# Latent attention: a depthwise convolution as 128x32 products of four shifted copies, interleaved with the attention's head groups

## The chip, the cores and the metric

The kernel runs on one core of a Trainium2 chip. The engines of the core work side by side, each with an instruction queue of its own that is executed in order: TensorE (PE) multiplies and transposes, VectorE (DVE), ScalarE (ACT) and GpSimd (POOL) do elementwise work, SyncE (SP) issues most of the DMAs. The metric is the device time of one execution in microseconds (us), as the median of several runs.

## The reference

Two transformer blocks of width 1024, one after the other, over 256 tokens in float32: a token mixer with a feed-forward part and a mixture of experts (MoE), twice a pair; then, in two layers, a feed-forward part, a mixing part and a second feed-forward part, and a norm. The change touches the mixing part of these two layers:

```python
p = h @ w_in[l]                                   # 384 + 256 + 32 + 2 * 512 columns
attn = mla_group(p[..., :o_kv], p[..., o_kv:o_pe], p[..., o_pe:o_cv], ...)
conv = conv_group(p[..., o_cv:], ...)
x = x + concatenate([attn, conv], axis=-1) @ w_out[l]
...
def mla_group(c_q_raw, c_kv_raw, k_pe_raw, ...):  # 8 heads, 64 + 32 of q and k, 64 of v
    q = (rms_norm(c_q_raw, q_lat_g) @ w_uq).reshape(b, s, 8, 96)
    kv = (rms_norm(c_kv_raw, kv_lat_g) @ w_ukv).reshape(b, s, 8, 128)
    # k = 64 of kv with the 32 of k_pe_raw for every head; q, k normed per head; rope on the 32
    # causal by chunks of 64: softmax(q k / sqrt(96)) v
def conv_group(u_raw, conv_w, conv_b, ln_g, ln_b):
    u = a * sigmoid(g)                            # the two halves of u_raw
    y = causal depthwise convolution of u, 31 taps, 512 channels, + conv_b
    return silu(layer_norm(y, ln_g, ln_b))
```

## The kernel before

The program goes through ten stages in this order: mix0, ffn0, mix1, moe, f1_0, mla0, f2_0, f1_1, mla1, f2_1. mla0 and mla1 are the mixing parts above; f1 and f2 are the feed-forward parts around them. Tokens lie in two tiles of 128 (t = 0, 1), X being the residual.

**Weights.** All of them are streamed from HBM by SP, in the order of `plan_...`, as blocks of 1 MB into a ring of four (`raw`); each block is cut into a high part `wh` by ACT (L237) and a low part `wl` by DVE (L238). A projection (`mul`) makes three products for each: high by high, low by high, high by low (L395, L396, L398), 128x128 of activations against up to 512 columns of weights. Activations are cut in the same way (`cut2`: ACT makes the high part `xhl`, DVE the low one). Before a stage the residual is transposed and cut and a reciprocal root of its mean square is made by `rstd_of`: two POOL instructions, L378 (add) and L379 (power). Behind the MoE there is one norm more: DVE scales X by that root (L440, `Norm.turn`), and only then X is transposed, cut and projected.

**Order.** A scheduler in the tile framework sets the order in each engine's queue from the order in which the code is written and from priorities (`tc.high_priority`), and puts the waits where data or buffers need them. It may put an instruction far ahead of where it is written, if its inputs and its buffer are there. A tile of PSUM (`bank`) or of SBUF that is asked for under a name in use makes its first writer wait for the last reader of the old one.

**A mixing stage** (`mla`) projects `ca` and `cg` (the two halves of u), `cq`, `ck` (latents of q and of k, v), then `uq` and `ukv` from the normed latents; q and k are normed per head (squares on ACT, sums on DVE, root on POOL), q's and k's last 32 columns are rotated by `rope` (L765 to L770, six products and sums on POOL for each t), heads are transposed by PE (L880) and moved by ACT; scores (L910, L911), exponentials (ACT L919), transposes of them (L404), values (L926). The out projection takes the attention half first and then the convolution's half, whose layer norm and silu (L946 to L956) are placed beside the first.

**The convolution** works on `uT`, u transposed to channels on partitions (four chunks of 128 channels) with 30 zero columns ahead. Chunks 0 and 1 and 26 taps of chunk 2 are done by DVE, one instruction a tap (`tap`, L788, L790). The remaining 5 taps and chunk 3 are 36 products of PE with a 128x128 diagonal that ACT makes from the identity for each tap (`pe_conv`, L796, L797). All of it has a low priority.

## Time and profile before

| | us |
|---|---|
| median of 3 runs | 2318.45 (2315.61 to 2323.34) |
| the profiled execution | 2321.03 |
| its span from first to last instruction | 2319.3 |
| mla0 and mla1, from the first to the last product of each | 134.3 and 131.6 |
| PE busy over the span | 2238.7 (97%) |
| DVE, ACT, POOL busy over the span | 926.1, 792.6, 172.7 |

Times in the rows are from the span's start. PE's products are pipelined, so a product's time overlaps with the next, and a busy PE isn't a PE at its full rate: the granted clock (PEclk, 1.00 is 2.4 GHz, 0.50 is 1.2 GHz) stands beside it. A float32 product leaves two records. The median of the runs is 2.6 us below the profiled execution, from which all rows come.

### The profile page before, as it was taken

How to read it: one execution, taken by the hardware profiler on the slowest of the kernel's cores; microseconds unless marked ns; L12 is line 12 of the kernel's file. 1: busy time of each engine (PE TensorE's matmuls, PEld its weight loads, DVE VectorE, ACT ScalarE, POOL GpSimd, SP SyncE). 2: the span in 40 equal slices, each digit the busy share in tenths (PEclk: the TensorE clock that was granted, in tenths of full speed). 3: DMA queues.
4: the chain of work that ended last, by engine and by line, in shares of the span. 5: the costliest groups of instructions: out<-in, count | busy, mean ns of one | idle time of the engine just before them, and what ended most of it. 6: DMA issues, size and time to landing. Idle time of an engine off the chain costs nothing. (4 is left out here: it accounts for less than half of the span.)

```text
span 2319.3 us, 36153 instructions
## 1 busy us (share of the span) xinstructions
PE 2238.7 (97%) x15276; PEld 1482.4 (64%) x15276; DVE 926.1 (40%) x1246; ACT 792.6 (34%) x1243; POOL 172.7 (7%) x258
## 2 busy tenths in 40 slices
PE   8999999899999999998999999989999999989998
PEld 7888888523433333333332688877888888867887
DVE  6655456201010101011010655586554645686544
ACT  5444444201010101101010544475444544575443
POOL 3000003000000000000000200061000100150000
PEclk9999999899999999999999999999999999999999
DMA  7655554899979999999999655441555555423552
GB/s 269 226 187 182 184 208 156 321 420 419 412 321 388 399 418 419 420 418 420 420 409 415 226 190 185 141 146 65 199 182 183 182 192 186 142 108 119 184 188 82
DMA packets 89436, 599.09 MB, mean 258 GB/s; under 512 B 12092, under 2 KB 14558, under 8 KB 18460
## 3 DMA queue, kind: packets, MB, share of 16 engines
q1 hardware_dynamic: 88956, 595.81, 66.2%
q8 instruction: 144, 2.36, 0.4%
q10 hardware_dynamic: 288, 0.52, 0.1%
q14 instruction: 48, 0.39, 0.0%
HBM read 595.25 MB, written 1.05 MB: 257 GB/s over the span
## 5 line engine op out<-in xcount | busy, mean ns | idle before, releaser
L238 DVE TENSOR_TENSOR wl<-raw,wh 128x1024 fp32r<-128x1024 f32 (+2 forms) x456 | 540.5, 1215 | 431.1 <-ACT wh L237 430.7
L237 ACT ACTIVATE wh<-raw 128x1024 fp32r<-128x1024 f32 (+2 forms) x456 | 454.6, 1036 | 485.8 <-PE mm L398 302.1
L1098 PE MATMUL mm<-raw,xe 128*32 128x512 f32 (+1 forms) x5376 | 506.8, 524 | 5.9 <-DMA raw<-in_w_moe_dram 5.1
L395 PE MATMUL mm<-wh,xhl 128*128 128x512 f32 (+3 forms) x1280 | 473.2, 372 | 2.3 <-ACT xhl L414 2.3
L396 PE MATMUL mm<-wl,xhl 128*128 128x512 f32 (+3 forms) x1280 | 471.5, 371 | 0.0
L398 PE MATMUL mm<-wh,xhl 128*128 128x512 f32 (+3 forms) x1280 | 394.4, 371 | 0.3 <-DVE xhl L415 0.3
L1098 PEld LDWEIGHTS mm<-raw,xe 128*32 128x32 f32 x5376 | 168.9, 110 | 301.5 <-issue 245.2
L1103 DVE TENSOR_TENSOR gs<-mm,gs 128x256 f32<-128x256 f32 (+1 forms) x84 | 31.2, 380 | 669.8 <-ACT gs L1102 420.9
L1126 PE MATMUL acc<-raw,gT 128*32 128x512 f32 (+1 forms) x2688 | 280.6, 523 | 12.4 <-DMA raw<-in_w_moe_dram 4.1
L395 PEld LDWEIGHTS mm<-wh,xhl 128*128 128x128 f32 x1280 | 241.8, 189 | 43.3 <-ACT xhl L414 2.7
L396 PEld LDWEIGHTS mm<-wl,xhl 128*128 128x128 f32 x1280 | 241.7, 189 | 40.9 <-DVE wl L238 0.6
L398 PEld LDWEIGHTS mm<-wh,xhl 128*128 128x128 f32 x1280 | 236.9, 189 | 41.5 <-DVE xhl L415 1.5
L1102 ACT ACTIVATE gs<-mm 128x256 f32<-128x256 f32 (+1 forms) x84 | 29.3, 349 | 516.3 <-PE mm L1098 516.3
L1126 PEld LDWEIGHTS acc<-raw,gT 128*32 128x32 f32 x2688 | 90.0, 109 | 168.2 <-issue 128.3
L395 PE MATMUL acc<-wh,ghl 128*128 128x512 f32 x464 | 186.0, 401 | 0.0
L396 PE MATMUL acc<-wl,ghl 128*128 128x512 f32 x464 | 183.4, 395 | 0.0
L398 PE MATMUL acc<-wh,ghl 128*128 128x512 f32 x464 | 145.3, 393 | 0.0
L378 POOL TENSOR_SCALAR s<-s 128x1 f32<-128x1 f32 (+1 forms) x60 | 32.3, 539 | 1156.5 <-ACT junk L385 1052.6
L398 PEld LDWEIGHTS acc<-wh,ghl 128*128 128x128 f32 x464 | 87.3, 188 | 20.7
L396 PEld LDWEIGHTS acc<-wl,ghl 128*128 128x128 f32 x464 | 87.6, 189 | 19.0
L395 PEld LDWEIGHTS acc<-wh,ghl 128*128 128x128 f32 x464 | 87.5, 189 | 18.7
L1112 ACT ACTIVATE gT<-mm 128x256 f32<-128x256 f32 (+1 forms) x84 | 29.1, 347 | 202.7 <-PE mm L1110 201.4
(254 smaller groups left out, 1633.0 us busy)
## 6 DMA issues: line engine op xcount, KB each, us to landing
raw<-in_w_moe_dram SPq DMA_DIRECT2D x336, 1024.0 KB
raw<-in_w_f_dram SPq DMA_DIRECT2D x132, 1024.0 KB
raw<-in_w_ffn_dram SPq DMA_DIRECT2D x42, 1024.0 KB
raw<-in_w_mix_dram SPq DMA_DIRECT2D x23, 1024.0 KB
raw<-in_w_mla_dram SPq DMA_DIRECT2D x18, 1024.0 KB
raw<-in_w_mla_dram SPq DMA_DIRECT2D x8, 576.0 KB
raw<-in_w_mla_dram SPq DMA_DIRECT2D x4, 768.0 KB
c<-in_cst_dram SPq DMA_DIRECT2D x2, 1024.0 KB
```

Source lines behind the costliest of these rows:

```text
L237: self.nc.scalar.activation(h[:, s], t, AF.Copy)
L238: self.nc.vector.tensor_tensor(l[:, s], t, h[:, s].bitcast(F32), op=ALU.subtract)
L378: nc.gpsimd.tensor_scalar(r, ms, EPS, None, ALU.add)
L395: nc.tensor.matmul(o, sh[:, k, :], h[:, j, a:b], start=first and i == 0, stop=False)
L396: nc.tensor.matmul(o, sh[:, k, :], l[:, j, a:b], start=False, stop=False)
L398: nc.tensor.matmul(o, sl[:, k, :], h[:, i + (r[0] if r else 0), a:b], start=False, stop=last and i == n - 1)
L1098: nc.tensor.matmul(ps[32 * j:32 * j + 32, :n], xe[e // 2][:, k, e % 2, 32 * g:32 * g + 32], units[k // 2][0](k % 2, c * n, n), start=k == ...
L1102: nc.scalar.activation(s, v[:, :, 0], AF.Silu)
L1103: nc.vector.tensor_tensor(s, v[:, :, 1], s, op=ALU.mult)
L1112: nc.scalar.activation(a, ps[:, :n * 128].rearrange("p (q c) -> p q c", q=n), AF.Copy)
L1126: last = nc.tensor.matmul(o[32 * j:32 * j + 32, :w], a[:, k % n, at:at + 32], units[k // 2][0](k % 2, c * w, w), start=b == 0 and k == 0, ...
```

## The change

The order of the projections becomes cq, ck, ca, uq, ukv, cg, and the convolution's half of the out projection comes first. The convolution moves to PE altogether. `uT` has no zero columns any more and lies in the scratch tile `junk`; SP copies it by 40 DMAs a layer, from SBUF to SBUF, into `us`: for each group of 32 channels a tile with those channels four times over its 128 partitions, each copy shifted by one token more. One product of a 128x32 weight with 256 columns then sums four taps of 32 channels, and eight products a group make the 32 taps (the first is zero). The four groups of a chunk go to the four column strips of the array. The weights (`taps`, 128x1024 a chunk, four chunks a layer, two buffers) are made on POOL from a sum of the identity's four blocks (`eye`) and the taps, which the host lays out (`cw` is loaded, not transposed at the start). The result `cv` goes into the scratch tile that `uT` had, by ACT. `rope` goes from POOL to DVE, as does one scaling of the norms; the copy of the transposed exponentials (`pT`) goes from ACT to DVE. Scores, values and the four parts of the convolution are written out as one interleaved list.

```diff
-        cols(("ca", l), w, 672, 512, D, 512)
-        cols(("cg", l), w, 1184, 512, D, 512)
         cols(("cq", l), w, 0, 384, D, 512)
         cols(("ck", l), w, 384, 288, D, 512)
+        cols(("ca", l), w, 672, 512, D, 512)
         for i in range(2):
             add((("uq", l), i), ("w_uq_2", (l,)), 0, 384, 384 * i, 384)
         add((("ukv", l), 0), ("w_ukv_2", (l,)), 0, 256, 0, D)
-        for i in range(4):
+        cols(("cg", l), w, 1184, 512, D, 512)
+        for i in (2, 3, 0, 1):
...
-        c["uT"] = pool.tile([128, 4, T + TAPS - 1], F32, name="uT")
-        nc.gpsimd.memset(c["uT"][:, :, 0:TAPS - 1], 0.0)
...
+        eye = c["eye"] = pool.tile([128, 32], F32, name="eye")
+        nc.gpsimd.tensor_tensor(eye, ident[:, 0:32], ident[:, 32:64], op=ALU.add)
+        for i in (2, 3):
+            nc.gpsimd.tensor_tensor(eye, eye, ident[:, 32 * i:32 * i + 32], op=ALU.add)
...
+    def taps_of(l, i, c, pool):
+        n = [128, 32, 32]
+        d = pool.tile(n, F32, tag="taps", name="taps", bufs=TABLES)
+        nc.gpsimd.tensor_tensor(d, c["eye"].unsqueeze(1).to_broadcast(n), cw[:, l, i].unsqueeze(2).to_broadcast(n), op=ALU.mult)
+        return d
...
-        e = nc.gpsimd
+        e = nc.vector
...
-        def pe_conv(i, k0):
-            ps = bank("acc")
-            for k in range(k0, TAPS):
-                d = pool.tile([128, 128], F32, tag="diag", name="diag", bufs=4)
-                nc.scalar.activation(d, ident, AF.Copy, scale=cw[:, l, i, k:k + 1])
-                nc.tensor.matmul(ps[:, :T], d, uT[:, i, k:k + T], start=k == k0, stop=k == TAPS - 1)
-            if k0:
-                nc.vector.tensor_tensor(cv[i], ps[:, :T], cv[i], op=ALU.add)
-            else:
-                nc.scalar.activation(cv[i], ps[:, :T], AF.Identity, bias=gain("conv_b_2", l)[:, i:i + 1])
...
-                with tc.high_priority(offset=-600):
-                    for k in range(TAPS):
-                        for j in range(3):
-                            if j < 2 or k < SPLIT:
-                                tap(j, k)
-                    pe_conv(2, SPLIT)
-                    pe_conv(3, 0)
...
+        ps_g = project(("cg", l), 2, nin, 512, K2, "acc")
+        gated = []
+        for t in range(2):
+            b = tp.tile([128, 512], F32, tag="g32", name="ug", bufs=4)
+            nc.scalar.activation(b, ps_g[t], AF.Sigmoid, scale=nin.r[t])
+            nc.vector.scalar_tensor_tensor(b, ps_a[t], nin.r[t], b, ALU.mult, ALU.mult)
+            gated.append(b)
...
+        wide = T + 28
+        us = [(xp.tile([128, UNIT], F32, tag="x", name="us")[:, :7 * wide].rearrange("p (g t) -> p g t", g=7),
+               pool.tile([128, 1, wide], F32, name=f"us{i}")) for i in range(2)]
+        for u in us:
+            for v in u:
+                nc.gpsimd.memset(v[:, :, 0:31], 0.0)
+        uT = tp.tile([128, 4, T], F32, tag="junk", name="uT", bufs=1)
+        for t in range(2):
+            p = turn4([gated[t][:, j * 128:(j + 1) * 128] for j in range(4)])
+            if t:
+                nc.vector.tensor_copy(uT[:, :, t * 128:(t + 1) * 128], p)
+            else:
+                nc.scalar.activation(uT[:, :, t * 128:(t + 1) * 128], p, AF.Copy)
+        for i in range(2):
+            for s in range(4):
+                n = min(T, wide - 31 + s)
+                for g in range(4):
+                    a = uT[32 * g:32 * g + 32, 2 * i:2 * i + 2, :n]
+                    k = 1 if g == 3 else 2
+                    nc.sync.dma_start(us[i][0][32 * s:32 * s + 32, 2 * g:2 * g + k, 31 - s:31 - s + n], a[:, :k])
+                    if g == 3:
+                        nc.sync.dma_start(us[i][1][32 * s:32 * s + 32, :, 31 - s:31 - s + n], a[:, 1:])
+
+        def group(i, g):
+            n = 2 * g + i % 2
+            return us[i // 2][0][:, n] if n < 7 else us[i // 2][1][:, 0]
+
+        def conv(i):
+            tab = taps_of(l, i, c, pool)
+            if i % 2 == 0:
+                sums.append(bank("acc"))
+            o = sums[i // 2][:, (i % 2) * T:(i % 2 + 1) * T]
+            for m in range(8):
+                for g in range(4):
+                    nc.tensor.matmul(o[32 * g:32 * g + 32], tab[:, 8 * g + m], group(i, g)[:, 4 * m:4 * m + T], start=m == 0, stop=m == 7)
+            nc.scalar.activation(cv[:, i // 2, i % 2], o, AF.Identity, bias=gain("conv_b_2", l)[:, i:i + 1])
...
-                nc.scalar.activation(pT, pp, AF.Copy)
...
+            nc.vector.tensor_copy(pT, pp)
...
+        css = quarters(F32)[0]
+        scores(0, 0)
+        cv = tp.tile([128, 2, 2, T], F32, tag="junk", name="cv", bufs=1)
+        conv(0)
+        scores(0, 1)
+        heads_T(kT, kf[1], 1, 1)
+        conv(1)
+        values(0, 0)
+        scores(1, 0)
+        values(0, 1)
+        a0 = weighted(0)
+        conv(2)
+        scores(1, 1)
+        conv(3)
+        values(1, 0)
+        b0 = conv_norm(0)
+        scores(1, 2)
+        attended(0, a0)
+        values(1, 1)
+        b1 = conv_norm(1)
+        scores(1, 3)
+        conv_out(0, b0)
+        values(1, 2)
+        conv_out(1, b1)
+        out_conv(0)
+        values(1, 3)
+        a1 = weighted(1)
+        out_conv(1)
+        attended(1, a1)
+        finish([(("wo2", l), 0), (("wo2", l), 1)], y, ch, cl, [range(0, 2), range(2, 4)], nout)
```

What the scheduler makes of it shows at three places.

POOL around the end of moe and the start of f1_0, before: `s_19671` is the mean square of X for t = 1, L378 and L379 make its root, on which DVE's scaling of X waits.

```order
L743 MEMSET neg 1x64
L745 MEMSET low 1x64
L746 MEMSET low 1x64
L756 MEMSET uT 128x4x30
L378 TENSOR_SCALAR s_19671<-s_19668 128x1
L379 TENSOR_TENSOR s_19671<-s_19671,mhalf 128x1
L754 TENSOR_TENSOR rot<-c_81,rg 128x16 x16
```

POOL there now; the same root is that of `s_19664` (lines L382, L383).

```order
L747 MEMSET neg 1x64
L749 MEMSET low 1x64
L750 MEMSET low 1x64
L761 TENSOR_TENSOR eye<-c_81 128x32
L887 MEMSET us_21565 128x31
L887 MEMSET us_21567 128x31
L763 TENSOR_TENSOR eye<-eye,c_81 128x32 x2
L769 TENSOR_TENSOR taps<-eye,cw 128x1024
L382 TENSOR_SCALAR s_19664<-s_19661 128x1
L769 TENSOR_TENSOR taps<-eye,cw 128x1024
L383 TENSOR_TENSOR s_19664<-s_19664,mhalf 128x1
L758 TENSOR_TENSOR rot<-c_81,rg 128x16 x16
```

Between the constants and the root now stand the sums for `eye`, two memsets of `us` and the first two tables; the second table is between the root's two halves.

SP at the end of mla0's weights, before: the last blocks of mla0, the first of f2_0 (`in_w_f_0`), then two small loads for mla1.

```order
L217 DMA raw<-in_w_mla_dram 128x1536 x2
L217 DMA raw<-in_w_mla_dram 128x1152 x4
L217 DMA raw<-in_w_mla_dram 128x2048 x5
L217 DMA raw<-in_w_f_0_dram 128x2048 x3
L741 DMA rg<-in_q_norm_dram 128x32
L741 DMA rg<-in_k_norm_dram 128x32
L217 DMA raw<-in_w_f_0_dram 128x2048 x2
```

SP there now, as far as the first half of the copies (an `x3` row is three DMAs).

```order
L226 DMA raw<-in_w_mla_dram 128x2048 x7
L226 DMA raw<-in_w_f_0_dram 128x2048 x2
L901 DMA us<-uT 32x2x253 x3
L901 DMA us<-uT 32x253
L903 DMA us_21565<-uT 32x253
L901 DMA us<-uT 32x2x254 x3
L901 DMA us<-uT 32x254
L903 DMA us_21565<-uT 32x254
L901 DMA us<-uT 32x2x255 x3
L901 DMA us<-uT 32x255
L903 DMA us_21565<-uT 32x255
L901 DMA us<-uT 32x2x256 x3
```

The copies stand in one row behind the first two blocks of f2_0; the other half follows in the same form (`us_21567`), and all of f2_0's later blocks behind it.

PE in mla0 where the convolution runs, before, in the middle of the heads: `diag` are products of the convolution, `kv,t32` values, `gn` transposes of exponentials, `kT,qT` scores.

```order
L797 MATMUL acc<-uT,diag 128x256 x2
L926 MATMUL acc<-kv_21585,t_21849 128x64 x4
L797 MATMUL acc<-uT,diag 128x256 x2
L404 MATMUL mm<-c_81,gn 128x128 x2
L910 MATMUL mm<-kT_21725,qT_21723 128x256
L404 MATMUL mm<-c_81,gn 128x128 x2
L911 LDWEIGHTS low
L911 MATMUL mm<-neg,low 128x64
```

PE now, with the numbers of the buffers: `us_21564` is the first set of copies (chunks 0 and 1) and `us_21566` the second (chunks 2 and 3); the `taps` are those of chunk 0 (`21646`), 2 (`21785`) and 1 (`21710`); `acc_21648` is the bank of chunks 0 and 1.

```order
L916 MATMUL acc_21648<-us_21564,taps_21646 32x256 x30
L916 MATMUL acc_21787<-us_21566,taps_21785 32x256 x2
L975 MATMUL acc_21866<-kv0_21292,t32_21872 128x64
L975 MATMUL acc_21866<-kv1_21293,t32_21872 128x64
L916 MATMUL acc_21787<-us_21566,taps_21785 32x256
L975 MATMUL acc_21866<-kv0_21292,t32_21872 128x64
L975 MATMUL acc_21866<-kv1_21293,t32_21872 128x64
L916 MATMUL acc_21787<-us_21566,taps_21785 32x256 x2
L916 MATMUL acc_21648<-us_21564,taps_21710 32x256 x3
L916 MATMUL acc_21648<-us0_21565,taps_21710 32x256
```

Chunk 0 ends here, five products of chunk 2 come next, and then chunk 1, whose bank is that of chunk 0. Before chunk 1 writes, ACT has moved chunk 0 out of the bank into `cv`, which stands where `uT` was. Between the end of chunk 0 and these products PE has only values to do. The out projection of the stage stands behind all parts of the convolution and the heads; before, its attention half stood ahead of the convolution's norm.

## Rows read from the trace of the kernel before

**Rows 1.** Windows of the two attention stages, mla1 first.

```profile
1992.64:2124.24 131.60, 118.83 (x632) 99.98 (x631) 95.96 (x179) 82.66 (x168) 38.35 (x50) 0.97 0.30 108
1481.48:1615.82 134.34, 121.78 (x631) 102.47 (x630) 96.16 (x179) 84.05 (x172) 44.41 (x70) 0.95 0.31 106
```

Columns: stretch, its length, busy time (and records) of PE, PEld (weight loads), DVE, ACT, POOL, granted clock, DMA share, GB/s.

**Rows 2.** Timeline of PE, mla0 and one row of mla1, with waits.

```profile
1536.21 1.08 PE L880 MATMUL mm<-c,q 128*96 128x128 f32 x8 [1.14 <-POOL q L770]
...
1541.42 2.00 PE L797 MATMUL acc<-uT,diag 128*128 128x256 f32 x8 [2.40 <-ACT diag L796]
...
1549.20 1.91 PE L880 MATMUL mm<-c,k 128*96 128x128 f32 x8 [5.79 <-DVE k L895]
...
2060.36 1.91 PE L880 MATMUL mm<-c,k 128*96 128x128 f32 x8 [5.78 <-DVE k L895]
```

Columns: start, duration, engine, line, operation; in brackets the idle time ahead and what ended it.

**Rows 3.** Windows of 5 us behind the long wait of each stage.

```profile
1550.00:1555.00 5.00, 4.92 (x28) 4.06 (x26) 3.11 (x10) 3.85 (x7) 2.07 (x2) 0.67 0.02 5
...
2060.00:2065.00 5.00, 4.64 (x19) 3.86 (x20) 3.12 (x9) 2.86 (x5) 2.06 (x2) 0.50 0.01 2
```

**Rows 4.** Timeline of POOL at the start of f1_0.

```profile
1297.78 0.22 POOL L378 TENSOR_SCALAR s<-s 128x1 f32<-128x1 f32 x1
1298.09 0.57 POOL L379 TENSOR_TENSOR s<-s,mhalf 128x1 f32<-128x1 f32 x1
```

**Rows 5.** Timeline of DVE there.

```profile
1298.69 1.29 DVE L440 SCALAR_TENSOR_TENSOR X<-X,s,post 128x1024 f32<-128x1024 f32 x1 [0.24 <-POOL s L379]
```

**Rows 6.** Timeline of PE there.

```profile
1300.66 0.73 PE L398 MATMUL mm<-wh,xhl 128*128 128x512 f32 x2 [0.30 <-DVE xhl L415]
```

**Rows 7.** PE's groups by form: count | busy us, mean ns of one | idle.

```profile
L1098 PE MATMUL mm<-raw,xe 128*32 128x256 f32 x1792 | 106.4, 380 | 0.2 <-DVE X L1157 0.2
...
L797 PE MATMUL acc<-uT,diag 128*128 128x256 f32 x144 | 39.1, 404 | 4.8 <-ACT diag L796 4.8
```

**Rows 8.** Groups of DVE and ACT from 1480 to 1640 us.

```profile
L790 DVE SCALAR_TENSOR_TENSOR cv<-uT,cw,cv 128x256 f32<-128x256 f32 x85 | 36.6, 488 | 0.0
...
L796 ACT ACTIVATE diag<-c,cw 128x128 f32<-128x128 f32 x36 | 12.9, 397 | 3.8 <-PE acc L797 3.4 <-ACT diag L796 0.2
```

**Rows 9.** Two lines of POOL: duration ns min/median/max, first and last start.

```profile
L637 POOL TENSOR_TENSOR vn<-vn,lg x4: 1297/1304/2145, 25.8 to 353.6; 128x512 f32<-128x512 f32 x4
...
L754 POOL TENSOR_TENSOR rot<-c,rg x32: 215/220/1259, 1298.6 to 1604.2; 128x16 f32<-128x16 f32 x32
```

**Rows 10.** Timeline, last product of `cg` and the copies of `uT`.

```profile
1503.95 0.39 PE L398 MATMUL mm<-wh,xhl 128*128 128x512 f32 x1
...
1509.16 1.07 ACT L811 ACTIVATE uT<-mm 128x512 f32<-128x512 f32 x2
```

**Rows 11.** Timeline of SP's queue: issues of small loads, near the start and in mla0.

```profile
47.13 0.42 SPq L311 DMA_DIRECT2D rows<-in_group_g_dram  x1
...
49.08 0.42 SPq L311 DMA_DIRECT2D rows<-in_ffn_norm_dram  x1
...
1595.98 0.33 SPq L741 DMA_DIRECT2D rg<-in_q_norm_dram  x1
```

**Rows 12.** Timeline of POOL, the first use of that load.

```profile
1598.86 3.27 POOL L754 TENSOR_TENSOR rot<-c,rg 128x16 f32<-128x16 f32 x11 [1.08 <-DMA rg<-in_q_norm_dram]
```

**Rows 13.** Timeline of DVE: statistics of the second convolution tile, last cut.

```profile
1595.87 0.70 DVE L948 BATCH_NORM_STATS2 s<-mm 128x6 f32<-128x512 f32 x1 [1.19 <-PE mm L946]
...
1603.13 0.70 DVE L415 TENSOR_TENSOR xhl<-ghl,xhl 128x512 fp32r<-128x512 f32 x1
```

**Rows 14.** Timeline of ACT, the table load ahead of the silu.

```profile
1592.88 1.28 ACT L956 ACT_TABLE_LOAD   x1
```

**Rows 15.** Timeline of PE, two products of 512 columns at full clock.

```profile
1503.27 0.39 PE L398 MATMUL mm<-wh,xhl 128*128 128x512 f32 x1
1503.50 0.39 PE L395 MATMUL mm<-wh,xhl 128*128 128x512 f32 x1
```

**Rows 16.** The issue of one more kind of load on SP: ns min/median/max.

```profile
L606 SPq DMA_DIRECT2D pw<-in_pool_w_dram x8: 465/575/889, 18.8 to 92.5; - x8
```

More of the change, by code (lines that the diff above doesn't have):

```diff
@@ L331, in model @@
     qkg = const.tile([QK, 4], F32, name="qkg")
[L332 removed]
+    cw = const.tile([128, 2, 4, 32], F32, name="cw")
     def parameters(pool):
@@ new lines, in scores @@
+            h0 = i * per
+            if i == 0:
+                st_[t] = [small(8) for _ in range(3)]
+            rs, mx, nm = st_[t]
+            ps = bank()
+            for i in range(per):
+                b = i * nk * 128
+                j, h = divmod(h0 + i, 4)
+                nc.tensor.matmul(ps[:, b:b + nk * 128], qT[j][:, h, t * 128:(t + 1) * 128], kT[j][:, h, 0:nk * 128], start=True, stop=False)
+                nc.tensor.matmul(ps[:, b + nk * 128 - 64:b + nk * 128], c["low"], c["neg"], start=False, stop=True)
@@ new lines, in values @@
+        def values(t, i):
+            nk = t + 1
+            per = 4 // nk
+            h0 = i * per
+            if i == 0:
+                o[t] = bank("acc")
+            p = p_.pop((t, h0))
+            pp = turn4([p[:, i * 128:(i + 1) * 128] for i in range(4)])
+            pT = tp.tile([128, 4, 128], F32, tag="t32", name="t32")
+            nc.vector.tensor_copy(pT, pp)
+            for i in range(per):
+                for k in range(nk):
+                    nc.tensor.matmul(o[t][:, (h0 + i) * 64:(h0 + i + 1) * 64], pT[:, i * nk + k, :], kv[k][:, h0 + i, 64:128],
+                                     start=k == 0, stop=k == nk - 1)
```

194 lines of the change are left out of this document (80 added, 114 removed).

## The prediction

> **What bounds the kernel now.** I read the stages first. The two attention stages take 134.34 and 131.60 us, and TensorE (PE) is busy for 121.78 and 118.83 of these [rows 1]; the rest, 12.6 and 12.8 us, is idle, and that is all a better order can win back directly. The timeline of PE shows where it sits: 1.14 us for the rotated q of GpSimd (POOL), 2.40 for a diagonal of ScalarE (ACT), and 5.79 (5.78 in the second layer) for the normed k of VectorE (DVE) [rows 2]. Behind the long wait the granted clock is at half: 0.67 of full at 1550 to 1555 us, 0.50 at 2060 to 2065 [rows 3], where 4.64 busy us did 2.3 us of work. Over the whole stages the mean clock is 0.95 and 0.97 [rows 1]; busy time times clock is 115.7 and 115.3, so the same work takes 115.5 us at full clock in both. Elsewhere PE has no gap that this change could reach, but there is one place where it has hardly any slack: the start of f1_0, behind the MoE stage. POOL computes a reciprocal root there from 1297.78 to 1298.66 [rows 4], DVE waits for it by 0.24 us and scales X [rows 5], and PE waits 0.30 us for the low half that DVE then cuts [rows 6].
>
> **The convolution's products cost PE the same.** Removed are 36 products of 128x128 by 256 columns a layer. 144 records (two to a product) were busy 39.1 us over both layers [rows 7], 19.5 a layer, in part at half clock; at full clock records follow each other at half of 0.427 us, 15.4 a layer. Added are 128 products of 128x32 by 256 columns, four column strips of the array beside each other. The MoE has this very shape: 1792 records took 106.4 us [rows 7], 59.4 ns each, so 256 records take 15.2 us. Gain 0 to 4 us a layer, the upper part being the clock, which the sum below has by itself; I take 0. **Taken off** DVE are 85 taps that were busy 36.6 us, off ACT 36 diagonals with 12.9 us [rows 8]. Neither engine limits these stages (they are busy some 96 and 84 of 134 us [rows 1]), so this is worth only what it shortens of the waits.
>
> **f1_0 pays for the tables.** POOL's order puts three sums for `eye`, two memsets and two `taps` tables of 128x1024 ahead of the reciprocal root on which DVE and PE wait. POOL's 128x512 product took 1.304 us in the median and its 128x16 one 0.220 [rows 9]: 2.19 ns an element, so a table is 2.42 us, an `eye` sum 0.25. Two tables, three sums, one more memset and the 0.1 us between instructions make 6.2 us. The same 128x512 product took 2.145 us beside a busy DVE, which would make a table 4.0 and the sum 9.4; but DVE stands still here, waiting. Nothing on PE is left to run: in the rows of before its next product is the one that waits for the low half. So PE stops 6.2 us longer (4 to 9.4), and the clock follows: behind 5.78 us of idleness the second layer ran five us at 0.50 [rows 3]. That is 2.3 more. **Loss 8.5 us, once**; in the second layer the tables stand in a stretch where no wait for POOL is near.
>
> The Trainium skill (GPSIMD Engine Reference, section "Performance versus the Vector engine") gives 2.6 cycles an element for a product of two tensors, at 1.2 GHz an estimate of 2.2 us a table, and tells to keep elementwise work on VectorE; the rows above agree in rate, and by its figure the sum is 5.8 in place of 6.2 us. It speaks against the tables on this engine, not against their being made.
>
> **The attention stage, by its chain.** Let E be the end of the last gate product. Before, the stage runs without idleness from 1481.48 until 1535.07; take off the transposes of u and four convolution products that lie in there (2.7 us) and the same projections end after 50.9 us. New in them is that latents are cut while the second query block waits for its weights' cut on ACT, about 1.6 us: E is 52.5 us from the start. The gate is now the last projection, so everything of the convolution begins at E. From the last gate product to the end of the second copy of `uT` it is 5.9 us now (1504.34 to 1510.23) [rows 10]; I take 6.5, since DVE and ACT have the head norms too. Then SP issues 40 copies. Rows of parameters, the nearest in kind, follow each other at 0.49 us [rows 11] (five issues, 47.13 to 49.08), and a small load is used 2.9 us after its issue (1595.98 [rows 11], POOL starts at 1598.86 [rows 12]). With 0.48 us each, `us[0]` has landed at E + 6.5 + 19 x 0.48 + 2.9 = E + 18.5 and all 40 at E + 28.1. Until E + 18.5 PE transposes heads and does scores, and still waits three times for the q and k norms, 4.4 us in sum by the same steps that made 1.14 + 2.40 + 5.79 [rows 2]: the rope is off POOL's slow queue, but on DVE it stands ahead of the same two POOL steps. conv(0) runs to E + 22.3. Now the written order (0, 1, 2, 3) isn't what PE executes: it has five products of conv(2) ahead of conv(1), these need the second set of copies, and conv(1) needs the bank's eviction, which writes `cv` into the buffer of `uT` and so waits until all 40 copies have read it. So PE stops until E + 28.1, less about 1 us of values: 4.8 us idle. Then 0.6 + 3.8 + 3.2 us, 0.5 for conv(2)'s eviction and 3.8 for conv(3): E + 40. The tail was hidden behind half of the out projection; now nothing fills it. From the statistics of a transposed tile to the last cut of its output took 8.0 us (1595.87 to 1603.83) [rows 13]; with transposes and eviction ahead of it (1.1) and two more table loads of 1.28 us [rows 14], as Silu and Exp now alternate on ACT, it is 12 us, some 5 of them idle. Out projection: 96 products at 0.23 us [rows 15], 21.8, and 1.1 for what follows: E + 75. Stage 127.5 us at full clock, 130 with the 2.5 us of half clock that the second layer shows behind a wait of such length. Counted the other way, the 115.5 us of work, 16.3 us of idleness (1.6 + 4.4 + 4.8 + 0.5 + 5) and 2.5 of clock make 134.3. I take 133 in both layers, nearer to the second, since the chain leaves out what PE loses at each change of operation: 1.3 us less than now in the first, 1.4 more in the second. **Sum 0** (-6 to +6).
>
> **Sum.** 2321.0 us (the profiled execution) + 8.5 + 0 = 2329.5; the median of the runs shown is 2.6 us below that execution, so **2327 us**. A measurement here tells about 0.3%, 7 us, from no change: above 2325.4 counts as slower.
>
> **Rivals.**
> (a) *Copies come early, faster.* If SP issues a copy each 0.33 us, as the load at 1595.98 took [rows 11], all have landed at E + 22, just when conv(0) ends. The 4.8 us go, the clock stays up and the tail starts earlier: 124 us a stage, 18 less in both, less 8.5: 2309. It decides from a spacing of 0.38 us down. For it: these are the shortest issues that the trace has. Against it: they are of one small contiguous load; copies of 64 rows of strided halves are nearer to the parameters' rows.
> (b) *Copies come late, slower.* The `pw` loads, also strided pieces, take 0.575 us in the median and up to 0.889 to issue [rows 16]. At 1 us, with waits between, the last lands at E + 48.4: 20 us more a layer, about 2370. [...]
> The Trainium skill (DMA: Bandwidth & Descriptors, section "Anatomy of one DMA") puts a fixed 2.0 us on each transfer whatever its size, which speaks against forty transfers of 64 KB. One behind the other they would take an estimate of 86 us and the stage 60 more. It also says that this is mostly completion latency, and the 0.49 us above show issues overlapping, so I give the serial reading nothing beyond this rival.
> (c) *The wait at f1_0 is absorbed* (tables faster, or started while POOL idles before the stage ends): 2318, no change. For it: POOL has little else to do ahead of it; against it: its queue is in order, and the rows ahead of `eye` wait for the MoE's end.
>
> **Chances.** The forecast 0.45, (a) 0.22, (b) 0.13, (c) 0.20. The forecast's own range is 2317 to 2340, from the bounds of f1_0 (4 to 12 with clock) and of the stages (-6 to +6). For 8 in 10 it must reach into (a) and part of (b): 2303 to 2352. Faster: most of (a) and half of (c), 0.25; within 0.3%: 0.29; slower: 0.46.
>
> **What would show it.** In f1_0, PE waiting some 6.5 us for the low half with POOL in two `taps` before it, and half clock behind; if that wait is under 2 us, (c). In the attention stages: SP's 40 issues and their spacing; PE idle between conv(0) and the five products of conv(2), released by a copy; PE idle in front of the out projection; stages of 127 to 139 us. Stages at 124 or less mean (a), at 150 or more (b). The prediction is wrong in its main step if PE goes from conv(0) to conv(1) without a wait, or if the strips cost other than 15 us a layer.

## The result, and the profile after

| | before | after |
|---|---|---|
| median of the runs, us | 2318.26 (2315.61 to 2323.34, 4) | 2339.51 (2337.14 to 2339.65, 4) |
| ratio, 95% interval | | 1.0082 (1.0067 to 1.0096) |
| span of the profiled execution, us | 2319.3 | 2335.4 |

Slower, as forecast, and inside the range; but the loss is 21 us where the likeliest case had 9. Cut at the places where PE starts to transpose X for the next stage, the two profiled executions differ like this:

| stretch | before, us | after, us | difference |
|---|---|---|---|
| start to the end of moe | 1287.7 | 1279.3 | -8.4 |
| f1_0 | 190.1 | 197.6 | +7.5 |
| mla0 | 134.4 | 140.9 | +6.5 |
| f2_0 and f1_1 | 376.8 | 376.8 | 0.0 |
| mla1 | 131.6 | 142.3 | +10.6 |
| f2_1 to the end | 198.7 | 198.7 | 0.0 |

The differences add up to 16 us, not to 21: the profiled execution of before lies 2.8 us above its median and that of after 2.4 below, and where these 5 us sit no row shows. The predicted terms were 0, +8.5, -1.3, 0, +1.4 and 0. So the term of f1_0 is right, those of the attention stages are not, and a gain in front hides part of it.

**f1_0.** The timeline of POOL after, at the place of [rows 4]:

```profile
1290.11 1.91 POOL L769 TENSOR_TENSOR taps<-eye,cw 128x1024 f32<-128x1024 f32 x1
1292.11 0.22 POOL L382 TENSOR_SCALAR s<-s 128x1 f32<-128x1 f32 x1
1292.41 1.91 POOL L769 TENSOR_TENSOR taps<-eye,cw 128x1024 f32<-128x1024 f32 x1
1294.28 0.57 POOL L383 TENSOR_TENSOR s<-s,mhalf 128x1 f32<-128x1 f32 x1
```

The timelines of DVE and of PE there, which answer to [rows 5, 6], and the windows behind:

```profile
1294.88 1.28 DVE L444 SCALAR_TENSOR_TENSOR X<-X,s,post 128x1024 f32<-128x1024 f32 x1 [4.83 <-POOL s L383]
```

```profile
1296.84 1.22 PE L402 MATMUL mm<-wh,xhl 128*128 128x512 f32 x2 [5.15 <-DVE xhl L419]
```

```profile
1295.00:1300.00 5.00, 3.16 (x8) 2.51 (x9) 4.73 (x5) 1.15 (x2) 5.00 (x8) 0.62 0.00 0
1300.00:1305.00 5.00, 5.00 (x17) 4.03 (x16) 2.36 (x2) 2.42 (x3) 3.91 (x12) 0.70 0.52 210
```

The root's second half ends behind the second table, DVE's wait grows from 0.24 to 4.83 us, PE's from 0.30 to 5.15, and the mean clock of the two windows is 0.62 and 0.70. A table takes 1.91 us. The windows over the whole of f1_0, those of before first, with one of 5 us near its start:

```profile
1287.70:1477.82 190.12, 189.82 (x892) 158.31 (x893) 104.19 (x106) 86.75 (x107) 17.59 (x31) 0.98 0.52 188
1290.00:1295.00 5.00, 5.00 (x16) 3.90 (x15) 5.00 (x8) 3.88 (x6) 1.84 (x4) 0.61 0.58 211
```

And after:

```profile
1279.29:1476.88 197.59, 191.96 (x893) 159.34 (x894) 103.61 (x106) 85.08 (x103) 19.32 (x37) 0.97 0.49 175
```

PE's idle time grows by 5.3 us, from 0.3 to 5.6. The kernel before, too, enters f1_0 at half clock (0.61), so half clock costs 2.0 us more than before, not the whole of what the two windows of after show.

**The attention stages.** Windows over both stages of the kernel after, mla0 first; they answer to [rows 1]:

```profile
1476.88:1617.73 140.85, 125.78 (x815) 98.32 (x814) 69.13 (x121) 72.28 (x134) 30.21 (x54) 0.94 0.35 122
1994.48:2136.74 142.26, 131.12 (x816) 100.92 (x814) 68.76 (x121) 72.28 (x134) 21.55 (x28) 0.90 0.35 120
```

Read them in three parts. Length less busy time is idle; busy time times mean clock is the work at full clock; the rest is what half clock costs. (The clock has two digits and is a mean over idle time too, so the last two are good to about 1 us.)

| | idle | half clock | work |
|---|---|---|---|
| before, mla0 / mla1 | 12.6 / 12.8 | 6.1 / 3.6 | 115.7 / 115.3 |
| after, mla0 / mla1 | 15.1 / 11.1 | 7.5 / 13.1 | 118.2 / 118.0 |

DVE lost 27 busy us a layer, ACT 12 and 10, and nothing of it arrives. In mla0 the 6.5 us are 2.5 of idle time, 2.5 of work and 1.4 of half clock. In mla1 the 10.6 us are 9.5 of half clock and 2.7 of work, less 1.7 of idle time. The timeline of PE in mla0, from the last gate product on:

```profile
1532.52 0.39 PE L402 MATMUL acc<-wh,xhl 128*128 128x512 f32 x1
...
1551.04 0.62 PE L916 MATMUL acc<-us,taps 128*32 128x256 f32 x2
...
1554.21 3.65 PE L916 MATMUL acc<-us,taps 128*32 128x256 f32 x60
1564.73 1.61 PE L916 MATMUL acc<-us,taps 128*32 128x256 f32 x4 [6.87 <-DMA us<-uT]
...
1578.81 3.66 PE L916 MATMUL acc<-us,taps 128*32 128x256 f32 x64
...
1597.34 0.78 PE L399 MATMUL acc<-wh,xhl 128*128 128x512 f32 x1
```

conv(0) starts at E + 18.1 (E, the end of the last gate product, is 1532.9) and, with products of the values between, ends at E + 25.0. Then PE stops until E + 31.8, when the first copies that conv(2) needs have landed. From the end of the last strip product (1582.5) to the out projection it is 14.9 us. At full clock 60 records take 3.65 us, 61 ns each. The timeline of SP, of which the first two rows and the last one stand here, and the row of ACT that moves conv(0) out of its bank:

```profile
1538.81 2.67 SPq L901 DMA_DIRECT2D us<-uT  x4
1541.53 0.59 SPq L903 DMA_DIRECT2D us<-uT  x1
...
1565.05 0.59 SPq L903 DMA_DIRECT2D us<-uT  x1
```

```profile
1567.17 0.47 ACT L917 ACTIVATE cv<-acc,g_q_latent_norm 128x256 f32<-128x256 f32 x1 [15.10 <-DMA us<-uT]
```

40 issues take 26.8 us, 0.67 each. ACT's eviction, which has to wait for all 40 copies, starts 2.1 us after the last issue, at E + 34.3. In mla1 the wait has another name:

```profile
2076.62 5.92 PE L916 MATMUL acc<-us,taps 128*32 128x256 f32 x60
2084.60 1.24 PE L916 MATMUL acc<-us,taps 128*32 128x256 f32 x4 [2.06 <-POOL taps L769]
```

```profile
2082.64 1.91 POOL L769 TENSOR_TENSOR taps<-eye,cw 128x1024 f32<-128x1024 f32 x1 [30.52 <-PE acc L916]
```

Here conv(0) took 5.92 us for the 60 records of 3.65, and it ended when the copies were nearly there. The third table can't be made before the first one's buffer is free (POOL starts it when conv(0) has ended), so PE waits for it. The windows of 5 us show why conv(0) was slow:

```profile
1537.00:1542.00 5.00, 4.92 (x29) 3.39 (x28) 3.72 (x5) 3.66 (x5) 0.00 (x0) 1.00 0.20 59
1540.00:1545.00 5.00, 4.80 (x24) 3.40 (x22) 2.65 (x5) 4.20 (x14) 0.00 (x0) 0.70 0.33 86
...
2060.00:2065.00 5.00, 2.30 (x13) 1.17 (x11) 1.20 (x3) 4.50 (x18) 0.00 (x0) 0.92 0.28 73
2065.00:2070.00 5.00, 5.00 (x16) 2.79 (x16) 1.55 (x4) 1.20 (x4) 0.00 (x0) 0.50 0.32 84
2070.00:2075.00 5.00, 5.00 (x18) 2.93 (x17) 0.79 (x3) 1.20 (x4) 0.00 (x0) 0.50 0.31 79
2075.00:2080.00 5.00, 5.00 (x40) 3.09 (x44) 1.38 (x2) 0.00 (x0) 0.00 (x0) 0.50 0.31 79
```

In mla1 the clock is at half from 2064 to 2080 and PE is busy all that time. In both layers the fall comes in the stretch of the heads' transposes and scores. What PE did just before is not the same: ahead of mla0's it was busy for 4.92 of 5 us, ahead of mla1's it had waited 1.04 and 1.66 us for ACT and was busy for 2.30 of 5.

### The profile page after: what moved, and what is told of

It is laid out like the page before. It is cut to its first block, busy times and chain, and to the rows that moved or that the text cites. A ratio compares the mean times of both kernels' runs of the same rounds, so it can differ in the third digit from the quotient of the medians.

```text
span 2335.4 us, 36775 instructions
## 1 busy us (share of the span) xinstructions
PE 2251.6 (96%) x15640; PEld 1476.6 (63%) x15640; DVE 870.3 (37%) x1133; ACT 768.1 (33%) x1167; POOL 143.0 (6%) x226
## 5 line engine op out<-in xcount | busy, mean ns | idle before, releaser
L247 DVE TENSOR_TENSOR wl<-raw,wh 128x1024 fp32r<-128x1024 f32 (+1 forms) x456 | 539.1, 1213 | 445.1 <-ACT wh L246 444.7
L246 ACT ACTIVATE wh<-raw 128x1024 fp32r<-128x1024 f32 (+1 forms) x456 | 453.9, 1035 | 493.8 <-PE mm L402 286.7
L399 PE MATMUL mm<-wh,xhl 128*128 128x512 f32 (+3 forms) x1216 | 448.4, 371 | 2.5 <-ACT xhl L418 2.5
L400 PE MATMUL mm<-wl,xhl 128*128 128x512 f32 (+3 forms) x1216 | 447.2, 370 | 0.5 <-DVE wl L247 0.5
L402 PE MATMUL mm<-wh,xhl 128*128 128x512 f32 (+3 forms) x1216 | 370.3, 371 | 5.1 <-DVE xhl L419 5.1
L399 PEld LDWEIGHTS mm<-wh,xhl 128*128 128x128 f32 x1216 | 230.2, 189 | 41.2 <-ACT xhl L418 2.9
L400 PEld LDWEIGHTS mm<-wl,xhl 128*128 128x128 f32 x1216 | 229.9, 189 | 39.2 <-DVE wl L247 1.3
L402 PEld LDWEIGHTS mm<-wh,xhl 128*128 128x128 f32 x1216 | 225.2, 189 | 44.1 <-DVE xhl L419 6.5
L382 POOL TENSOR_SCALAR s<-s 128x1 f32<-128x1 f32 (+1 forms) x60 | 24.9, 416 | 1125.2 <-ACT junk L389 1037.2
```

What stands on the lines that cost most here:

```text
L246: self.nc.scalar.activation(h[:, s], t, AF.Copy)
L247: self.nc.vector.tensor_tensor(l[:, s], t, h[:, s].bitcast(F32), op=ALU.subtract)
L382: nc.gpsimd.tensor_scalar(r, ms, EPS, None, ALU.add)
L399: nc.tensor.matmul(o, sh[:, k, :], h[:, j, a:b], start=first and i == 0, stop=False)
L400: nc.tensor.matmul(o, sh[:, k, :], l[:, j, a:b], start=False, stop=False)
L402: nc.tensor.matmul(o, sl[:, k, :], h[:, i + (r[0] if r else 0), a:b], start=False, stop=last and i == n - 1)
```

## The experiments

Twelve kernels ran, in four groups. Ratios are to runs of the kernel before that were taken beside each group; stages are read from each profile by the same marks as above.

| kernel | median, us | ratio (95%) | f1_0 | mla0 | mla1 |
|---|---|---|---|---|---|
| before | 2318.26 | | 190.1 | 134.4 | 131.6 |
| after | 2339.51 | 1.0082 (1.0067 to 1.0096) | 197.6 | 140.9 | 142.3 |
| t_late | 2332.21 | 1.0055 (1.0040 to 1.0071) | 190.9 | 140.7 | 142.8 |
| t_owncv | 2331.60 | 1.0051 (1.0034 to 1.0069) | 196.1 | 139.6 | 139.0 |
| b_cw | 2314.90 | 0.9980 (0.9970 to 0.9991) | 190.1 | 134.3 | 131.5 |
| b_rope | 2324.00 | 1.0019 (1.0004 to 1.0034) | 190.2 | 134.1 | 134.8 |
| t_fill | 2341.12 | 1.0094 (1.0080 to 1.0108) | 196.2 | 142.4 | 142.6 |
| t_first | 2332.32 | 1.0053 (1.0038 to 1.0067) | 197.2 | 139.6 | 136.1 |
| t_poolrope | 2338.37 | 1.0076 (1.0062 to 1.0091) | 197.3 | 140.5 | 142.2 |
| t_all | 2323.84 | 1.0008 (0.9985 to 1.0030) | 190.9 | 134.5 | 140.5 |
| t_all_fill256 | 2321.02 | 1.0014 (1.0003 to 1.0026) | 190.9 | 138.1 | 132.9 |
| t_all_fill | 2306.87 | 0.9945 (0.9931 to 0.9960) | 190.8 | 129.3 | 129.2 |
| t_all_fill4 | 2303.05 | 0.9933 (0.9916 to 0.9950) | 190.9 | 127.4 | 127.2 |
| b_cw_fill | 2333.14 | 1.0065 (1.0048 to 1.0082) | 190.1 | 140.9 | 141.2 |

**t_late: tables not before their stage.**

```diff
+        one = small()
+        nc.gpsimd.tensor_scalar(one, nin.r[0], 0.0, 1.0, ALU.mult, ALU.add)
+        eye = pool.tile([128, 32], F32, name="eye_late")
+        nc.gpsimd.tensor_tensor(eye, c["eye"], one.to_broadcast([128, 32]), op=ALU.mult)
+        c["eye"] = eye
```

> The kernel after, with the tables made from an eye that is multiplied by a one worked out from the stage's first root, so that POOL cannot make them before the attention stage has begun. Theory (the tables ahead of the root cost f1_0 its 7.5 us): PE's wait for the low half at the start of f1_0 falls from 5.15 to about 0.3 us, no half clock behind it, f1_0 7 to 8 us shorter, the whole about 2332. Rival (the tables only move their cost): two tables of 1.9 us each then stand in front of the head norms on POOL, the attention stages get 2 to 4 us longer each and the whole gains under 3 us.

f1_0 is back at 190.9 us, the attention stages are as long as they were, and the whole is at 2332.2 us, the number expected. The timeline of PE in this kernel, at the low half of f1_0:

```profile
1294.30 0.73 PE L402 MATMUL mm<-wh,xhl 128*128 128x512 f32 x2 [1.30 <-DVE xhl L419]
```

1.30 us are left of 5.15, where 0.3 were expected: the three `eye` sums and two memsets still stand ahead. The tables' place is the cause of f1_0's loss; made inside the attention stage they make it no longer (140.7 and 142.8 us for 140.9 and 142.3).

Inside mla0, though, something changed places. The windows of the stage and of its heads' stretch in this kernel, and PE's row behind conv(0):

```profile
1471.44:1612.10 140.66, 131.22 (x816) 102.87 (x815) 69.70 (x121) 72.35 (x134) 30.80 (x56) 0.89 0.35 123
...
1545.00:1550.00 5.00, 5.00 (x17) 2.66 (x16) 1.32 (x5) 2.40 (x8) 0.00 (x0) 0.50 0.27 68
1550.00:1555.00 5.00, 5.00 (x27) 3.28 (x30) 1.38 (x2) 0.00 (x0) 0.00 (x0) 0.50 0.28 72
```

```profile
1561.20 0.80 PE L922 MATMUL acc<-us,taps 128*32 128x256 f32 x4 [2.06 <-POOL taps L769]
```

Idle time is 9.4 us for 15.1 and half clock costs 14.4 for 7.5, with the order of the stage, its copies and its buffers untouched. The clock fell in the same stretch, but here it stayed at half into conv(0). PE came later to the place where the copies are needed, and there was no wait for them, only the one for the third table. So mla0 can pay the same 140.7 us in idle time or in clock.

**t_owncv: half of the convolution's result in its own buffer.**

```diff
-            nc.scalar.activation(cv[:, i // 2, i % 2], o, AF.Identity, bias=gain("conv_b_2", l)[:, i:i + 1])
+            nc.scalar.activation(cv[i // 2][:, i % 2], o, AF.Identity, bias=gain("conv_b_2", l)[:, i:i + 1])
...
-        cv = tp.tile([128, 2, 2, T], F32, tag="junk", name="cv", bufs=1)
+        cv = [pool.tile([128, 2, T], F32, name="cv0"), tp.tile([128, 2, T], F32, tag="junk", name="cv1", bufs=1)]
```

> The kernel after, with the convolution's result for chunks 0 and 1 in a buffer of its own instead of the scratch tile that the copies read; PE's order then has chunk 1 right behind chunk 0. Theory (PE stops for the copies because chunk 1 stands behind chunk 2 and the scratch tile): chunk 1 (3.8 us) runs inside the wait, which falls from 6.9 to about 3 us in mla0, and the half clock behind it gets shorter; 4 to 7 us less in mla0, 2 to 6 in mla1, the whole 2326 to 2334. Rival (only the last copy counts, and the clock): PE waits as long, only later; 0 to 2 us.

The edit did what it should to the order: chunk 1 stands right behind chunk 0, and PE waits for no copy any more. Yet the stages gain only 1.3 and 3.2 us (f1_0, which the edit doesn't touch, is 1.5 shorter too). The windows of 5 us in mla0 say why: ahead of the place where PE stood before, and into it, PE now works at half clock.

```profile
1550.00:1555.00 5.00, 5.00 (x17) 2.85 (x16) 1.14 (x5) 2.40 (x8) 0.00 (x0) 0.50 0.32 82
1555.00:1560.00 5.00, 5.00 (x30) 3.27 (x33) 1.38 (x2) 0.00 (x0) 0.00 (x0) 0.50 0.30 77
```

The whole, 2331.6 us, lies in the theory's range, but neither theory nor rival had the stages right. That the buffer took the wait away is not shown by this run: t_late lost the same wait in mla0 without it, PE being late at half clock. Of the kernels below, t_all_fill and t_all_fill4 have the buffer, full clock and no wait for a copy, but in another order of the stage.

**b_cw: the kernel before, with only the laid-out taps.** The transposes of the convolution's weights at the start and the copy behind them go; a load of the laid-out taps takes the place of the weights' load.

```diff
-        e.dma_start(c, A["conv_w_2"].rearrange("l k c -> (l k) c"))
+        e.dma_start(cw.rearrange("p l i c -> p (l i c)"), A["taps"])
...
-            for j in range(4):
-                nc.tensor.transpose(ps[:, j * 2 * TAPS:(j + 1) * 2 * TAPS], c[:, j * 128:(j + 1) * 128], ident[:2 * TAPS, :2 * TAPS])
```

> The kernel before, with the convolution's weights laid out by the host and loaded, in place of the transposes at the start; nothing else changed. The kernel after was 8.4 us ahead when it reached f1_0. Theory (this edit does it): the landmarks of mix0 come 1 and 3 us earlier as in the kernel after, and the whole gets 3 to 8 us faster. Rival (it is spread of the MoE stage from one execution to the next): 0 to 1 us, landmarks as before.

3.5 us faster. mix0 ends at 90.5 us in place of 93.4 (90.3 in the kernel after). That is the place of the edit, but its size isn't fixed by single profiles: the other kernels with the edit end mix0 between 90.3 and 92.5 us, and b_rope, which hasn't got it, at 92.7. The MoE stage is 870.8 us in place of 874.0, and it is between 868.6 and 871.1 in the profiles of ten of the eleven other kernels with this edit, against 873.6 and 874.0 in the two without: some 3 us more, for which no row gives a reason. mix1 is 1.5 us shorter in the kernel after (80.5 for 81.9) and not in this one; that part isn't explained either.

**b_rope and t_poolrope: the rope's engine alone, both ways.** The first is the kernel before with `e = nc.vector` in `rope` and the scaling of the root on DVE; the second the kernel after with both back on POOL.

> The kernel before, with the rope and one scaling of the norms on DVE in place of POOL; nothing else changed. Theory (POOL's slow rope is what makes PE wait 1.14 and 5.79 us): the wait for the normed k falls to 2 or 3 us and the half clock behind it goes, 3 to 8 us less in each attention stage, the whole 2305 to 2312. Rival (DVE has the taps too, and stands in the way as POOL did): the waits are then for DVE, the whole within 2 us of 2318.

> The kernel after with the rope and the scaling of the norms back on POOL; nothing else changed. Theory (on POOL the six steps of 128x128 are slow beside DVE and stand ahead of the roots): PE waits 4 to 8 us more for q and k, stages 4 to 10 us longer, the whole 2348 to 2360. Rival (in the new order the heads' chain has slack, as in the kernel before, where the same move made it no faster): within 3 us of 2339.

The theory fails both times. t_poolrope is the rival's case, 1 us from the kernel after. b_rope is not faster, but at 2324.0 us it is outside the rival's 2 us as well, and its longest wait is for ACT, not for DVE. The timeline of PE in mla0 of b_rope:

```profile
1543.07 1.22 PE L797 MATMUL acc<-uT,diag 128*128 128x256 f32 x2 [4.22 <-ACT diag L796]
1545.84 1.91 PE L880 MATMUL mm<-c,k 128*96 128x128 f32 x8 [1.55 <-DVE k L895]
```

The wait for k falls from 5.79 us [rows 2] to 1.55, and the one for a diagonal two steps ahead grows from 2.40 to 4.22; mla1 even gets 3.2 us longer, as its half clock costs 9.9 us (124.14 busy at 0.92) in place of 3.6. In the kernel after, rope on POOL costs nothing (2338.4 for 2339.5). So the rope's engine explains the wait for k, but taking that wait away only moves it to the diagonals, and it does not explain the result of the change.

**t_fill: more work for PE in the heads' stretch.**

```diff
             ps = bank()
+            nc.tensor.matmul(ps, ident, c0, start=True, stop=True)
             for i in range(per):
```

> The kernel after, with one more product ahead of each group of scores (128x128 by 512 columns in float32, about 0.85 us at full clock, six a layer); its result is overwritten by the scores. PE gets 5 us more work a layer. Theory (in the stretch of small transposes and scores PE works too little, the granted clock falls to half there and the convolution and values behind it run at half clock, 7.5 us in mla0 and 13 in mla1): the clock stays at 1.00 until conv(0), mla1 gets 3 to 8 us shorter in spite of the work, mla0 0 to 2. Rival (the clock falls because of the wait for the copies or goes down anyway): both stages get 4 to 6 us longer, the whole about 2350.

The windows of t_fill at the places where the kernel after had 0.70 and 0.50:

```profile
1540.00:1545.00 5.00, 5.00 (x28) 3.40 (x28) 2.77 (x5) 2.93 (x8) 0.00 (x0) 1.00 0.30 78
2065.00:2070.00 5.00, 4.22 (x17) 2.19 (x16) 2.14 (x5) 2.25 (x8) 0.00 (x0) 1.00 0.28 74
```

The clock stays at 1.00 until PE reaches the copies; then PE stops, and the clock falls to half at the end of that wait:

```profile
1565.21 1.63 PE L916 MATMUL acc<-us,taps 128*32 128x256 f32 x4 [5.87 <-DMA us<-uT]
...
2084.58 1.53 PE L916 MATMUL acc<-us,taps 128*32 128x256 f32 x4 [6.12 <-issue]
```

So the theory holds on the clock and fails on the time: mla1 gains nothing (142.6 for 142.3 us) and mla0 is 1.5 us longer. 5 us of work were added, and with PE at full speed the copies are late in both layers. Clock and copies hide each other. The filler also shortens the waits ahead of mla1's fall (0.18 and 0.78 us for 1.04 and 1.66), so this run alone doesn't tell whether its work or the shorter waits kept the clock.

**t_first: the attention half of the out projection ahead of the convolution's norm.** All scores and most values are written ahead of conv(0) to conv(3), then `attended`, the blocks 0 and 1 of the out projection, then (with priority) the norm and silu, and the blocks 2 and 3 last, as before the change.

> The kernel after, with scores and values written ahead of the convolution, and the attention half of the out projection ahead of the convolution's norm and half, as in the kernel before. Theory (the tail of norm, silu and table loads in front of the out projection, some 15 us with 5 to 6 us of idle PE and a spell of half clock, is exposed because nothing is left to run): the tail is covered, 5 to 8 us less in each stage, the whole 2325 to 2330. Rival (the tail's waits are not the loss, the clock in front of it is): 0 to 2 us.

1.2 and 6.2 us less in the stages. Windows of both:

```profile
1476.19:1615.82 139.63, 130.56 (x816) 102.65 (x815) 69.35 (x121) 69.57 (x132) 29.31 (x54) 0.89 0.36 123
1992.56:2128.66 136.10, 130.81 (x815) 102.47 (x814) 69.30 (x121) 69.57 (x132) 21.55 (x28) 0.89 0.37 126
```

Idle time falls by 6 us in each (to 9.1 and 5.3), and half clock rises to 14.4 in each. In mla0 that takes nearly all of it. The 6 us are not all where the theory had them. In mla0 the wait that went is the one for the copies, at half clock as in t_late, and a longer one came in the tail, for the convolution's norm:

```profile
1597.31 1.11 PE L408 MATMUL mm<-c,cn 128*128 128x128 f32 x4 [4.82 <-DVE cn L928]
```

In mla1 that wait is 0.52 us and the one for the third table is gone. Clock and copies again decide what the order is worth, and the whole, 2332.3 us, is short of the 2325 to 2330 expected.

**t_all: the three edits together.** t_late, t_owncv and the order of t_first, with conv(2) and conv(3) between the blocks of the out projection:

```diff
...
+        for i in range(2):
+            w.append(W.take((("wo2", l), i)))
+            for t in range(2):
+                mul(halves(y, t), ch[t], cl[t], range(2 * i, 2 * i + 2), w[i], i == 0, False)
+                if i == 0:
+                    conv(2 + t)
...
```

> The kernel after with three edits: tables not before the stage, an own buffer for half of the convolution's result, and the attention half of the out projection written ahead of chunks 2 and 3 and of the convolution's norm. Theory (the loss is these waits and the clock behind them): f1_0 back at 183 us, stages of 120 to 126 us, the whole 2300 to 2310, faster than both. Rival (the granted clock falls in the heads' stretch whatever follows): stages 130 to 134, the whole about 2315 to 2320.

Idle time is 5.3 and 5.6 us, there is no wait for a copy or a table, and still the kernel is no faster than the one before. Its executions run from 2301.6 us, at a mean clock of 0.994, to 2330.4 us, at 0.980. In the profiled one mla1 is 6 us longer than mla0, with the same 815 records on PE. The windows are those of the two stages, and one ahead of mla1's fall of the clock:

```profile
1471.02:1605.53 134.51, 129.19 (x815) 98.85 (x814) 70.25 (x121) 69.69 (x132) 33.55 (x56) 0.94 0.38 128
1982.24:2122.69 140.45, 134.87 (x815) 101.31 (x814) 70.26 (x121) 69.68 (x132) 26.95 (x32) 0.89 0.36 122
...
2042.00:2047.00 5.00, 4.92 (x31) 3.56 (x29) 3.62 (x5) 3.66 (x6) 0.00 (x0) 1.00 0.24 77
```

Work is 121.4 and 120.0 us and idle time the same; what differs is the clock, which fell at 2047 though PE had been busy for 4.92 of 5 us. This is the rival's case in its mechanism; its upper bounds, 134 us a stage and 2320 in all, were passed by 0.5 and 6.5 us and by 4.

**t_all_fill, t_all_fill256, t_all_fill4: the same with the filler.** The product of t_fill ahead of all six groups of scores; with 256 columns (`ps[:, :256]`, `c0[:, :256]`); and with 512 columns ahead of four groups (`if h0 < 4 + 4 * (t == 0)`).

> The kernel with the three edits (late tables, own buffer, attention half ahead) and one more 512-column product ahead of each group of scores, overwritten by them. In the profile of the three edits alone, half clock took about 8 busy us from mla0 and 15 from mla1, most of it between the first scores and the second chunk. Theory (that clock is all that keeps the three edits from their gain): at the price of 5 us of work a layer the stages are 129 to 132 us both, and equal from one execution to the next; the whole 2304 to 2312, faster than both kernels. Rival (with the clock up PE runs into the copies again, as it did with the same filler in the kernel after): a wait of 4 to 8 us for a copy, stages 134 to 138, no gain on 2324.

> The same with 256 columns in the filler, half its work (2.5 us a layer). Theory (PE only has to be kept at work): the clock stays up as with 512 columns, 2 us a stage less than with these. Rival (half the filler is too little): half clock in the heads' stretch in one layer or both, times spread as with the three edits alone.

> The kernel with the three edits and the 512-column filler, but ahead of four of the six groups of scores only (the two of t = 0 and the first two of t = 1): 1.7 us less work a layer. Theory (the clock has to be kept up until conv(0) and the values are reached, which lie behind the fourth group): the clock stays at 1.00, stages of 127 to 128 us, the whole 2302 to 2305. Rival (the last two groups need it as well): half clock behind them, stages of 131 to 138 and a wide spread, as with 256 columns.

With 512 columns no stretch of the attention stages is under 1.00, and both are 129 us; with four fillers 127.4 and 127.2, windows of both:

```profile
1472.72:1600.10 127.38, 121.91 (x823) 94.53 (x822) 70.09 (x121) 69.67 (x132) 33.74 (x56) 1.00 0.39 136
1976.85:2104.09 127.24, 121.88 (x823) 94.55 (x822) 70.11 (x121) 69.69 (x132) 26.94 (x32) 1.00 0.39 136
```

More work, less time: 3.4 us a layer of products that nobody reads save 7 and 13 us against the profile of t_all. The executions with 512 columns, six and four fillers, lie within 4.7 and 2.8 us of each other. t_all's fastest execution, without a filler, took 2301.6 us, and t_all_fill4's 2301.7: the filler makes no execution faster than the best of t_all, it keeps all of them there. With 256 columns half clock is back (138.1 and 132.9), the rival; whether it is the columns or the time they take that counts, no run separates. t_all_fill4 is the fastest kernel here, 0.9933 of the one before, of which b_cw's edit alone has 0.9980.

**b_cw_fill: the filler in the kernel before.**

> The kernel before with the laid-out taps and the same 512-column filler ahead of each group of scores (eight in this kernel: two for t = 0 and four for t = 1, six a layer); the convolution as it was. It asks whether the filler alone is worth what it brought to the changed kernel. Theory (here half clock costs only 4 to 6 us a layer, most of it behind a wait of 5.8 us that stays): the filler's 5 us are not won back, 0 to 3 us longer a stage, the whole 2315 to 2321. Rival (the clock is the loss in this kernel too): stages of 127 to 129 us, the whole 2304 to 2308, and the new convolution has no part in the gain.

18 us slower than b_cw, and the stages 6.6 and 9.7 us longer, more than the filler's 5. The windows give 14.1 and 14.3 us of idle time and 7.6 and 6.3 of half clock (126.76 busy at 0.94, 126.86 at 0.95). The waits of [rows 2] stay, and half clock stays with them. While they stay the filler is only work; the theory has the direction, its size was too small (0 to 3 us a stage). The rival, that the filler alone brings the gain, is out.

## Why the prediction was right, and where it was not

*f1_0 pays for the tables*: right, in mechanism and size. 8.5 us predicted, 7.5 measured, and t_late gives 6.7 of it back. A table took 1.91 us, not 2.42, so PE's idle time grew by 5.3 us and not 6.2; half clock cost 2.0 us more over the stage, where 2.3 were forecast. By the 2.6 cycles an element of the Trainium skill (GPSIMD Engine Reference, section "Performance versus the Vector engine") a table is an estimated 2.2 us; the trace has 1.91, 14% less.

*The convolution's products cost PE the same*: right. 61 ns a record at full clock, 59.4 predicted. The stages' work as a whole rose by 2.5 us on 115.5, which the sum had at 0; no run shows of what.

*By its chain*: right up to the start of conv(0) (E + 18.1 for 18.5; it ended at E + 25.0 for 22.3, with values between), and right that PE would go to chunk 2 next and stop for the copies. Copies were issued each 0.67 us and not 0.48, so that the last had landed by E + 34.3, not E + 28.1, which is part of rival (b); the wait in mla0 was 6.9 us for 4.8. The tail took 14.9 us for 12. What was not seen is that the third table waits for the first one's buffer, so in mla1 it is POOL that PE waits for. Altogether idle time was 15.1 and 11.1 us where this sum had 16.3. The fixed 2.0 us that the prediction cites from the Trainium skill (DMA: Bandwidth & Descriptors, section "Anatomy of one DMA") stands in that section for DMAs that GpSimd issues, and SP issued these. In the trace the last copy took 2.1 us from its issue to the eviction that waited for it, and the 40 took 28.4 in all, overlapping, not one behind the other.

*130 with the 2.5 us of half clock that the second layer shows behind a wait of such length*: this step failed, by its size. Half clock cost 7.5 and 13.1 us. The 2.5 us are the second layer's; the first had a wait of the same length (5.79 us [rows 2]) and lost 6.1 by [rows 1], so a larger term was at hand. And I had tied the clock to long waits, because before its longest fall stood beside one. In the kernel after it falls in the stretch of the heads' transposes and scores, where PE waits for at most 1.7 us at a time, and all that follows, conv(0) too, runs at half until it is back. In mla1 two such waits came just before (2.30 of 5 us busy); in mla0, and in mla1 of t_all, none did (4.92 of 5). t_fill shows that this stretch is the place: with one product of 0.85 us more in each group the clock keeps 1.00 through it. The Trainium skill (TensorE: Matmul & The Clock Gate, section "Part 1: The HAM clock gate") says that the gate follows how busy PE has been. The runs agree where PE waits (the fall beside 5.87 us of waiting in t_fill); where a stretch is busy in the trace they do not (4.92 of 5 us busy ahead of a fall, and then 5.00 of 5 at 0.50), so busy time as the trace counts it doesn't tell the clock.

*Sum 0* for the stages was therefore +17, outside its -6 to +6, and the stages (140.9 and 142.3 us) lie above the 127 to 139 that were to be its sign. The 8.4 us that the kernel after had won before f1_0, for which the prediction had no term, took half of the error away again. Without them the time would be an estimated 2348 us, still inside 2303 to 2352 but outside the forecast's own 2317 to 2340: that 2339.5 lies in that narrower range is luck. b_cw puts 3.5 us of the 8.4 on the laid-out taps; the rest is not explained.

*Rivals.* (a) did not come, as its condition, a spacing of 0.38 us or less, was missed. Its step that the clock stays up once the wait is gone is wrong: t_owncv and t_all have no wait for copies and stages of 134 to 140 us. Its price is not: at full clock and without that wait t_all_fill4 has 127.4 us with 3.4 us of filler, an estimated 124 without, in another order of the stage. (b) came in part, with 0.67 us a copy. (c) did not come: PE's wait was 5.15 us, not under 2.

## What to carry to other kernels

An engine freed is worth only the wait that ended on it, and a wait taken away is worth what the engine then does at the clock it gets: read idle time, work and half clock of a stage apart before choosing an edit. A stretch of small products can look fully busy and still lose the clock for the long products behind it. Here one product of 512 columns ahead of a group of scores kept the clock, and it paid only once the long waits were gone as well; try wide work there, useful if there is any, and see whether the profile's clock stays up. And a table that can be made at any time will be made at the earliest: give it something to depend on, so that it isn't ahead of a small result on which others wait.

## What was not expected of the hardware

- The same PE records in two layers of one execution took 134.5 and 140.5 us (t_all), with idle time and work equal to within 1.5 us and the granted clock at 0.94 and 0.89; with four fillers 127.4 and 127.2.
- The clock fell to half in a stretch where PE was busy for 4.92 of 5 us (after, mla0; t_all, mla1).
- A product of 128x1024 on POOL with both inputs broadcast took 1.91 us (1.87 ns an element), where 128x512 of two full tiles took 1.30 (2.5).
- 40 copies within SBUF, of 32 partitions by one or two rows, took SP 0.67 us each to issue in the mean, more than the parameters' loads (0.49), and that, not the 2.1 us behind the last issue, sets when the last one lands.
- The MoE stage was 868.6 to 871.1 us long in the profiles of eleven of the twelve kernels whose start had lost four small transposes and one copy, the kernel after among them, and 873.5 in the twelfth (t_all_fill), against 873.6 and 874.0 in the two that had kept them. Why was not found, and with 873.5 the lost work may not be the cause.
